# Layer 1 of a two-layer backbone: output weights split and stored in the V/z stage, key stores issued behind the last powers, the eighth weight block's splits issued behind evictions

## The chip, the cores and the metric

The kernel runs on one core of a Trainium2 chip. The core has a matrix engine (PE, with its weight loads shown apart as PEld), a vector engine (DVE), a scalar engine (ACT), a general engine (POOL) and SP, which in this kernel only issues DMA transfers. ACT and POOL issue some transfers too. Each engine works through its own instructions in order; a wait holds everything behind it on that engine. The metric is the device time of one execution in microseconds (us).

## The reference, cut to what matters

The program is a backbone of two layers over 2048 latent tokens of width 1024, with 256 context tokens, in float32. The change is in layer 1, which is a neighbourhood attention layer:

```python
def odd_mixer(h, hc, w_in, q_gain, k_gain, rpb, w_out, update_ctx):
    q, k, v, z = jnp.split(jnp.dot(h, w_in), 4, axis=-1)      # 16 heads of 64; likewise for the context tokens hc
    q, k = rms_norm(q, q_gain), rms_norm(k, k_gain)
    o = neighborhood_attention(q, k, v, k_ctx, v_ctx, rpb)     # 8 x 16 window of a 32 x 64 grid, and all 256 context keys
    y = jnp.dot(o * jax.nn.silu(z), w_out)                     # w_out: 1024 x 1024
# after it: x = x + gate * y
```

(`odd_mixer` is shortened here; the context tokens are not updated in the last layer.)

## The kernel before

**Numbers in two parts.** A float32 matrix is used as a sum of a high part (rounded by an ACT copy to the matmul format) and a low part (DVE: original minus high part). A product takes three matmuls: high x high, high x low, low x high (lines L129, L130 and L131). So each weight block has to be split once: a load into a staging tile `wraw`, an ACT copy (L106, out `w0h` to `w3h`), and a DVE subtraction (L391, out `w0l` to `w3l`).

**Stages of layer 1.** Tiles are 128 tokens: 18 of them, the first two being context. `odd_qk` multiplies the tiles with the weight blocks 0 to 3 of `w_od` (512 columns each: two for q, two for k) and at its end with block 4 (half of V) for the last two tiles. `odd_vz` does the rest of blocks 4 and 5 (V) and 6 and 7 (z). Then `odd_attention` runs eight head pairs, j = 0 to 7, some 47 us each, and ends with the output projection, token tile by token tile.

**`odd_qk`.** A cell is one token tile times one block, 24 matmuls into a PSUM tile `gm`. For q and k: ACT squares (`osq`), DVE sums (`oss`), POOL raises to the power -1/2 (`rpow`, L208 and L210), DVE multiplies (`onat`, L1159), PE transposes (L1167, `tp`), ACT and DVE split the result (`oqh`, `oql`; for keys also `okt`). For V (j = 4) ACT copies `gm` to `onat`, and POOL stores it (`store_v`). The keys are collected for groups of four token tiles in `okt` tiles. When a group is full, POOL stores it to DRAM (`store_k`, L1200): eight transfers of 512 KB for each of the four groups. A transfer that POOL issues stands in POOL's queue with its powers.

**Weight splits on the side.** Lists of steps wait in `self.ahead`. `pump` is called after each step of the matmul stream, and at every fourth call takes one step of the first list: two 128 x 512 pieces of a block. When the last cell of a block is done, `done(j)` appends the next block for the same buffers (blocks 4 to 7 go to the places w0 to w3). The staging tiles `wraw` have three buffers, so a load on SP waits until an earlier split is done. `held(steps)` runs steps so that what they issue comes behind the instruction in `self.evicted`.

**The order of instructions** on each engine is set by a planner. It works with estimated costs; `issue_after(x)` tells it to place what follows behind instruction x.

**`odd_vz`.** `weave` runs the V and z cells and, beside them, `maxes`: for 16 heads, PE multiplies queries with keys (`mx`), DVE adds a table of position biases (`mtab`, to which POOL has added a mask, L1279 and L1280) and takes the largest score of each row. SP loads the keys (`mk`, L1276), tables (L1278) and queries (`mq`, L1288); ACT reorders the queries (`mz`). `gm` has two banks here, `mx` five. The pools of this stage use the SBUF space of the pools of `odd_qk`.

**`odd_attention`.** For each head pair there are 16 latent steps (kind "l") and 4 context steps. Scores go to PSUM (`st`, L1390 and L1391), DVE adds the table (L1548, out `opt`), ACT exponentiates, PE multiplies with the values (`o`, L1402 and L1424), POOL sums the exponentials (`oacc`, L1430). `finish` divides by the sum and stores the result `rc` to the DRAM scratch `RT1`, by POOL. In the last pair, j = 7, the generator `weights` loads the output weights, 512 KB for each k of 0 to 7, into `opt` slots (of which there are 11), and `split` makes the two parts of them: 16 ACT copies and 16 DVE subtractions (L1075), each behind an exponential. The parts go to `wo0` and to buffers that are free by then: old q tiles, `ov`, `tab` and `kc` tiles. For the first token tile, z and all eight rows of `RT1` are loaded at n = 11, multiplied at n = 14 (L1578), split at n = 14 (ACT, `hi0`) and n = 15 (DVE, L1581, `lo0`); the projection begins with `first`.

Of the kernel before, what the change touches and what calls it, by code (L numbers as in the profile page):

```python
# [10 lines left out]
F32 = mybir.dt.float32  # L11
F32R = mybir.dt.float32r
# [5 lines left out]
P = 128  # L18
# [70 lines left out]
class Kern:  # L89
# [115 lines left out]
    def rpow(self, out, in_, mul, add):  # L205

        g = self.nc.gpsimd
        g.tensor_scalar(out=out, in0=in_, scalar1=mul, scalar2=add, op0=ALU.mult, op1=ALU.add)  # L208
        shp = list(out.shape)
        g.tensor_tensor(out=out, in0=out, in1=self.mhalf[:, : shp[1]], op=ALU.pow)  # L210

# [910 lines left out]
    def odd_qk(self, ws, win, hT):  # L1122
# [6 lines left out]
        with ExitStack() as es:  # L1129
# [5 lines left out]
            self.ahead += [self.od_steps(win, 0, ws), self.od_steps(win, 1, ws)]  # L1135
            pend, kt = [], {}

            def cell(t, j):
# [17 lines left out]
                nc.vector.tensor_reduce(out=ss[:], in_=sq[:].rearrange("p (h d) -> p h d", h=8), axis=AX.X, op=ALU.add)  # L1156
                self.rpow(ss[:], ss[:], 1.0 / 64, EPS)
                n = self.tl(sp, [P, 512], "onat", bufs=4)
                nc.vector.tensor_tensor(out=n[:].rearrange("p (h d) -> p h d", h=8), in0=ps[:],  # L1159
                                        in1=ss[:].unsqueeze(2).to_broadcast([P, 8, 64]), op=ALU.mult)  # L1160
                pend.append((t, j, n))

            def fin(t, j, n):
# [29 lines left out]
                if r0 == 6:  # L1193
                    store_k(kt.pop(j), j0, CTX + g * 512, 512)

            def store_k(parts, j0, o, w):

                for u, x in enumerate(parts):
                    for i in range(2):
                        nc.gpsimd.dma_start(self.K1t[j0 : j0 + 4, i, u * 64 : u * 64 + 64, o : o + w].rearrange("j d t -> d j t"),  # L1200
                                            x[i * 64 : i * 64 + 64].bitcast(F32))
# [22 lines left out]
    def odd_vz(self, ws, win, hT):  # L1224
        nc = self.nc
        self.z1 = self.scr("z1", (KD, P, SEQ), F32)
        self.M1 = self.scr("M1", (16, SEQ), F32)
        NR, NC = (len(b) for b in BLOCKS["q"])
        with ExitStack() as es:
# [6 lines left out]
            def cell(t, j):  # L1236
# [6 lines left out]
                if j < 6:  # L1243
                    self.act(n[:], ps[:])
                    self.store_v(t, j - 4, n)
                    return
# [24 lines left out]
            def maxes():  # L1271
# [51 lines left out]
    def odd_attention(self, out, right, left, wout):  # L1323
# [4 lines left out]
        with ExitStack() as es:  # L1328
# [109 lines left out]
            def weights():  # L1438

                for k in range(KD):  # L1440
                    if k == 0:
                        pl = [self.tl(left, [P, D], f"wo0{z}", F32R, bufs=1)[:] for z in "hl"]
                    elif k < 5:
                        q = qtile(8, k % 2, (k + 1) // 2)
                        pl = q[:, :D], q[:, D:]
                    elif k == 5:
                        v = self.tl(vp[0], [P, NT, P], "ov", F32R, bufs=1)[:].rearrange("p t d -> p (t d)")
                        pl = v[:, :D], v[:, D : 2 * D]
                    elif k == 6:
                        pl = [self.tl(tp[0], [P, NR, NC], f"tab{i}", F32R, bufs=1)[:].rearrange("p r c -> p (r c)")[:, :D] for i in range(2)]  # L1450
                    else:
                        pl = None
                    for n in range(2):
                        c = slice(n * 512, n * 512 + 512)
                        if pl:
                            wout[k, n] = [x[:, c] for x in pl]
                        else:
                            k1 = self.tl(kcp, [P, 2, CTX], "kc1", F32R, bufs=2)
                            wout[k, n] = [x[:].rearrange("p i c -> p (i c)") for x in (k1, ones["kc"].pop(0))]
# [15 lines left out]
            Q, kc, kt, V, tabs, raw = {}, {}, [], {}, {}, {}  # L1475
            Q[0, 1] = query(0, 1)
# [9 lines left out]
            mask(tabs[0])  # L1486
            out_w, out_s = weights(), split()
            pend, late, OA, first_sums = [], [], {}, {}
            FIRST_SUMS = {2: 1, 3: 1, 4: 0, 5: 0, 8: 2, 9: 2, 12: 3, 13: 3}
            all_k = slice(0, KD)  # L1490

            def flush(n):

                mm = None
                for f, *a in pend[:n]:
                    mm = f(*a)
                del pend[:n]
                for x in late:
                    x[0] -= 1
                for x in [x for x in late if x[0] <= 0]:  # L1500
                    late.remove(x)
                    finish_block(*x[1:])
                return mm

            for j in range(8):
                OA[j] = {}, {}
                for s, (kind, n) in enumerate(steps):
# [53 lines left out]
                    pend.append((tail_ctx if kind == "c" else tail, n, pts, j, V[j], *OA[j]))  # L1561
                    if j == 7 and 3 < s < 17:
                        with self.tc.issue_after(ex.ins):
                            next(out_s, None)
                    if j == 7 and n == 11:
                        z0, r0 = [exps([P, KD, P]) for _ in range(2)]
                        rows(z0, self.z1, 0, all_k)
                        rows(r0, self.RT1, 0, all_k)
                    elif j == 7 and n == 12:
# [4 lines left out]
                        hi0, lo0 = [exps([P, KD, P], F32R) for _ in range(2)]  # L1574
                    elif j == 7 and n in (14, 15):
                        with self.tc.issue_after(bias.ins):
                            if n == 14:
                                nc.vector.tensor_tensor(out=r0[:], in0=r0[:], in1=z0[:], op=ALU.mult)  # L1578
# [158 lines left out]
```

## Time and profile before

| | |
|---|---|
| median of 3 runs | 3652.93 us (3652.69 to 3655.3) |
| the profiled execution | 3652.31 us; span 3650.5 us; mean granted PE clock 0.988 |
| PE busy | 3552.0 us (97%), 18404 matmuls |
| DVE busy | 2355.2 us (65%) |
| ACT busy | 1433.2 us (39%) |
| POOL busy | 1234.9 us (34%) |
| `odd_qk` ends, `odd_vz` begins | 2621.0 us from the span's start |
| first matmul of the maxima | 2641.0 us |
| first matmul of the output projection | 3459.7 us |

The views show, for each engine, what was busy and what ended an idle time. In a timeline, a line has the start and the duration in us, the engine, the source line, the operation, out<-in, the shapes, and in brackets the idle time of that engine just before, with what released it. A matmul's duration overlaps with its neighbours; the distance from start to start is the pace. In a line of the waits stand the engine, its line, what it waited for, and the total, the number and the longest of these waits. In a line of the windows stand the stretch, its length, the busy time and number of instructions of PE, PEld, DVE, ACT and POOL, the clock that PE was granted (1.00 is full), the busy share of the 16 DMA engines, and GB/s.

### The profile page before, as it was taken

How to read it: one execution, taken by the hardware profiler on the slowest of the kernel's cores; microseconds unless marked ns; L12 is line 12 of the kernel's file. 1: busy time of each engine (PE TensorE's matmuls, PEld its weight loads, DVE VectorE, ACT ScalarE, POOL GpSimd, SP SyncE). 2: the span in 40 equal slices, each digit the busy share in tenths (PEclk: the TensorE clock that was granted, in tenths of full speed). 3: DMA queues.
4: the chain of work that ended last, by engine and by line, in shares of the span. 5: the costliest groups of instructions: out<-in, count | busy, mean ns of one | idle time of the engine just before them, and what ended most of it. 6: DMA issues, size and time to landing. Idle time of an engine off the chain costs nothing. (4 is left out here: it accounts for less than half of the span.)

```text
span 3650.5 us, 51811 instructions
## 1 busy us (share of the span) xinstructions
PE 3552.0 (97%) x18404; PEld 2747.6 (75%) x18404; DVE 2355.2 (65%) x4846; ACT 1433.2 (39%) x2740; POOL 1234.9 (34%) x1376
## 2 busy tenths in 40 slices
PE   8999999999999999999999999999899999999899
PEld 6988987888886666665656887888788887555577
DVE  4677666888876766678765435455488784666732
ACT  5445551111115555555654214444422222555510
POOL 1433330101011211221311224333344442888763
PEclk9999999999999999999999999999999999999999
DMA  7455463222243232342632544545734446898672
GB/s 259 142 156 155 135 177 110 87 75 84 69 116 86 66 107 66 89 125 66 179 110 93 184 139 141 159 146 155 245 126 144 131 133 181 212 223 220 190 235 97
DMA packets 365780, 512.25 MB, mean 140 GB/s; under 512 B 26081, under 2 KB 245297, under 8 KB 359618
## 3 DMA queue, kind: packets, MB, share of 16 engines
q1 hardware_dynamic: 320754, 417.69, 39.3%
q0 software_dynamic: 22112, 63.26, 5.7%
q10 hardware_dynamic: 22656, 27.99, 2.2%
q8 instruction: 146, 2.39, 0.3%
q14 instruction: 112, 0.92, 0.1%
HBM read 329.45 MB, written 179.37 MB: 139 GB/s over the span
## 5 line engine op out<-in xcount | busy, mean ns | idle before, releaser
L963 DVE TENSOR_TENSOR acc<-acc,apt 128x512 f32<-128x512 f32 x512 | 375.6, 756 | 168.5 <-ACT apt L106 165.6
L106 ACT ACTIVATE apt<-st 128x512 f32<-128x512 f32 (+1 forms) x592 | 343.6, 594 | 290.7 <-PE st L974 262.0
L660 DVE TENSOR_REDUCE mm<-mx 128x1 f32<-128x512 f32 (+1 forms) x656 | 388.7, 629 | 87.3 <-PE mx L659 80.0
L914 PE MATMUL av<-apt,av 128*64 128x512 f32 (+1 forms) x1184 | 280.6, 594 | 0.0
L972 PE MATMUL st<-aq,akh 97*128 97x512 f32 (+1 forms) x592 | 256.6, 434 | 8.8 <-DMA aq<-QT 4.4
L659 PE MATMUL mx<-mk,mq 96*128 96x512 f32 (+1 forms) x656 | 235.8, 373 | 5.0 <-DMA mq<-QT 3.4
L1430 POOL TENSOR_TENSOR oacc<-oacc,opt 128x576 f32<-128x576 f32 (+5 forms) x192 | 223.0, 1184 | 39.7 <-ACT rl L106 19.3
L973 PE MATMUL st<-aq,akh 96*128 96x512 f32 (+1 forms) x592 | 235.5, 398 | 0.0
L1548 DVE TENSOR_TENSOR opt<-st,tab 128x64 f32<-128x64 f32 (+10 forms) x576 | 144.6, 317 | 140.3 <-PE st L1391 63.8
L974 PE MATMUL st<-aq,akl 96*128 96x512 f32 (+1 forms) x592 | 234.4, 396 | 0.0
L106 ACT ACTIVATE u<-gm 128x352 f32<-128x352 f32 (+1 forms) x140 | 68.6, 498 | 373.2 <-PE gm L131 210.6
L1307 DVE CUSTOM_DVE_ANT_1 mx<-mx,mtab 128x217 f32<-128x217 f32 (+12 forms) x576 | 184.2, 338 | 40.1 <-PE mx L1301 30.9
L914 PEld LDWEIGHTS av<-apt,av 128*64 128x64 f32 x1184 | 80.5, 137 | 153.6 <-issue 152.3
L972 PEld LDWEIGHTS st<-aq,akh 97*128 97x128 f32 x592 | 113.0, 191 | 99.1 <-issue 50.5
L106 ACT ACTIVATE opt<-opt 128x930 f32<-128x930 f32 (+7 forms) x129 | 104.2, 810 | 110.7 <-DVE opt L1548 102.6
L659 PEld LDWEIGHTS mx<-mk,mq 96*128 96x128 f32 x656 | 121.2, 188 | 16.8 <-DMA mk<-KT 3.8
L974 PEld LDWEIGHTS st<-aq,akl 96*128 96x128 f32 x592 | 113.9, 193 | 25.6
L973 PEld LDWEIGHTS st<-aq,akh 96*128 96x128 f32 x592 | 114.4, 193 | 17.1
L129 PE MATMUL gm<-w1h,hhi 128*128 128x512 f32 x288 | 116.3, 404 | 6.8 <-ACT onat L106 6.8
L106 ACT ACTIVATE x<-px,modB,modA 128x128 f32<-128x128 f32 x272 | 99.3, 468 | 56.9 <-PE px L339 54.4
L129 PE MATMUL gm<-w0h,hhi 128*128 128x512 f32 x288 | 116.3, 404 | 2.0 <-DVE hhi L351 1.9
L807 POOL TENSOR_TENSOR gsf<-gsf,D 64x512 f32<-64x512 f32 x17 | 25.1, 1477 | 271.4 <-DVE D L784 271.4
(492 smaller groups left out, 9962.1 us busy)
## 6 DMA issues: line engine op xcount, KB each, us to landing
q<-Q SPq DMA_DIRECT2D x48, 512.0 KB
H<-x ACTq DMA_DIRECT2D x36, 512.0 KB
adaw<-ada_w SPq DMA_DIRECT2D x64, 256.0 KB
x<-H SPq DMA_DIRECT2D x32, 512.0 KB
wraw<-w_od SPq DMA_DIRECT2D x64, 256.0 KB
K1t<-okt POOLq DMA_DIRECT2D x32, 512.0 KB, 7.6
kt<-K1t SPq DMA_DIRECT2D x32, 512.0 KB
mtab<-rpb_q SPq DMA_DIRECT2D x16, 899.0 KB
```

Of the source, the lines that this page charges most:

```text
L106: return self.nc.scalar.activation(out, in_, func, **kw)
L129: self.nc.tensor.matmul(out, lh(k), rh(k), start=j == 0, stop=False)
L659: mm = nc.tensor.matmul(ps[:, :w], q[:A_QK, (t % 6) * P : (t % 6) * P + P], k[:A_QK, k0 : k0 + w], start=True, stop=True)
L660: nc.vector.tensor_reduce(out=m[:, t, n : n + 1], in_=ps[:, :w], axis=AX.X, op=ALU.max)
L914: nc.tensor.matmul(O[j, nb][i * 64 : i * 64 + 64, :w], V[j, kt // TT][:, kt % TT, i * 64 : i * 64 + 64], pts[i][:, :w], start=n == 0, stop ...
L963: nc.vector.tensor_tensor(out=acc[i][:, :w], in0=a[:, :w], in1=pts[i][:, :w], op=ALU.add)
L972: nc.tensor.matmul(ps[:, :w], kh[: A_QK + 1, i, kq], qh[: A_QK + 1, :w], start=True, stop=False)
L973: nc.tensor.matmul(ps[:, :w], kh[:A_QK, i, kq], ql[:A_QK, :w], start=False, stop=False)
L974: mm = nc.tensor.matmul(ps[:, :w], kl[:A_QK, i, kq], qh[:A_QK, :w], start=False, stop=True)
L1307: nc.vector.tensor_tensor_reduce(out=s, in0=s, in1=tb[:, ri : ri + rn, ci : ci + cn], scale=1.0, scalar=-3e38, op0=ALU.add, op1=ALU.max, a ...
L1430: self.psum = nc.gpsimd.tensor_tensor(out=a, in0=a, in1=pts[:, :, a0 - r0 : a1 - r0, :], op=ALU.add)
L1548: bias = nc.vector.tensor_tensor(out=pt[:, d[0], d[1]], in0=ps[:, d[0], d[1]], in1=tabs[j][i][:, ri : ri + rn, ci : ci + cn], op=ALU.add)
```

## The change

There are three parts.

1. In `odd_qk`, the eight key stores of the last group (g = 3) are kept in a list `last` and issued behind the power of the last cell, (17, 1); `rpow` returns that instruction. The splits of the eighth block (j = 7, place w3) come from `late()`: four empty steps, then `held`, so that they stand behind the V copies (`self.evicted`, set in `odd_qk` and `odd_vz`).
2. In `odd_vz`, a new generator `output_weights` is appended to `self.ahead`. After 16 empty steps it loads 16 pieces of 128 x 512 of the output weights (256 KB each, into `wraw` tiles), splits each by an ACT copy and a DVE subtraction, and has POOL store both parts to a DRAM scratch `WO`; five empty steps follow each piece.
3. In `odd_attention`, j = 7, `split` is gone. `weights` loads both parts from `WO` straight to their places (8 MB in all instead of 4 MB). For the first token tile only the rows k < 7 are loaded from `RT1` and multiplied, at n = 13; the last eighth is taken from the tile that `finish` returns (`done_rows[0, 7]`), at n = 14, ahead of `hi0`.

```diff
-        g.tensor_tensor(out=out, in0=out, in1=self.mhalf[:, : shp[1]], op=ALU.pow)
+        return g.tensor_tensor(out=out, in0=out, in1=self.mhalf[:, : shp[1]], op=ALU.pow)
...
-                    self.act(n[:], ps[:].rearrange("p h d -> p (h d)"))
+                    self.evicted = self.act(n[:], ps[:].rearrange("p h d -> p (h d)"))
...
+                if (t, j) == (NT - 1, 1):
+                    with self.tc.issue_after(power.ins):
+                        for x in last:
+                            store_k(*x)
...
                 if r0 == 6:
-                    store_k(kt.pop(j), j0, CTX + g * 512, 512)
+                    last.append((kt.pop(j), j0, CTX + g * 512, 512))
+                    if g < 3:
+                        store_k(*last.pop())
...
+            def late():
+                yield from range(4)
+                yield from self.held(self.od_steps(win, 7, ws))
+
             nxt = {2: 4, 3: 5, 0: 6, 1: 7}
-            done = lambda j: j in nxt and self.ahead.append(self.od_steps(win, nxt[j], ws))
+            done = lambda j: j in nxt and self.ahead.append(late() if j == 1 else self.od_steps(win, nxt[j], ws))
...
+        self.WO = self.scr("WO", (KD, P, 2, D), F32)
...
+            def output_weights():
+
+                yield from range(16)
+                for k in range(KD):
+                    for n in range(2):
+                        lo, hi = [self.tl(self.prp, [P, 1, 512], "wraw", dt, bufs=self.wbufs) for dt in (F32, F32R)]
+                        c = slice(n * 512, n * 512 + 512)
+                        nc.sync.dma_start(lo[:], self.i["w_out1"][:, k : k + 1, c])
+                        self.act(hi[:], lo[:])
+                        nc.vector.tensor_tensor(out=lo[:].bitcast(F32R), in0=lo[:], in1=hi[:], op=ALU.subtract)
+                        for z, x in enumerate((hi[:].bitcast(F32), lo[:])):
+                            nc.gpsimd.dma_start(self.WO[k, :, z, c], x[:, 0])
+                        yield from range(5)
+
+            self.ahead.append(output_weights())
...
                     if k == 0:
-                        pl = [self.tl(left, [P, D], f"wo0{z}", F32R, bufs=1)[:] for z in "hl"]
+                        x = self.tl(left, [P, 2, D], "wo0", F32R, bufs=1)[:]
...
+                    if k < 6:
+                        self.load(x.bitcast(F32), self.WO[k])
+                        x = [x[:, 0], x[:, 1]]
...
-                    raw[k] = exps([P, D])
-                    self.load(raw[k][:], self.i["w_out1"][:, k, :])
...
-            def split():
-                for k in range(KD):
-                    for n in range(2):
-                        hi, lo = wout[k, n]
-                        self.project_split(raw[k][:, n * 512 : n * 512 + 512], hi, lo)
-                        wout[k, n] = [x.unsqueeze(1) for x in (hi, lo)]
-                        yield
...
-                    finish_block(*x[1:])
+                    done_rows[tuple(x[1:3])] = finish_block(*x[1:])
...
-                    if j == 7 and 3 < s < 17:
-                        with self.tc.issue_after(ex.ins):
-                            next(out_s, None)
...
-                        rows(r0, self.RT1, 0, all_k)
+                        rows(r0, self.RT1, 0, most_k)
...
-                    elif j == 7 and n in (14, 15):
+                    elif j == 7 and n in (13, 14, 15):
                         with self.tc.issue_after(bias.ins):
-                            if n == 14:
-                                nc.vector.tensor_tensor(out=r0[:], in0=r0[:], in1=z0[:], op=ALU.mult)
+                            if n == 13:
+                                nc.vector.tensor_tensor(out=r0[:, most_k, :], in0=r0[:, most_k, :], in1=z0[:, most_k, :], op=ALU.mult)
+                            elif n == 14:
+                                nc.vector.tensor_tensor(out=r0[:, KD - 1, :], in0=done_rows[0, 7][:, :P], in1=z0[:, KD - 1, :], op=ALU.mult)
                                 self.act(hi0[:], r0[:])
...
-            for _ in out_s:
-                pass
```

On the engines' queues, the change leaves the number of matmuls and the order of most instructions as they were. At the end of `odd_qk` POOL has all powers first, then the eight key stores, then the V stores; ACT has the eight splits of block 6 (`w2h`) ahead of the last two `onat` copies and those of block 7 (`w3h`) behind them. In `odd_vz` the first matmuls of the maxima stand behind 39 instead of 29 matmuls with w2, and the 32 stores to `WO` fall into the first five of the sixteen heads. In j = 7 SP issues 12 loads from `WO` instead of 8 of `w_out`.

More of the change, by code (lines that the diff above doesn't have):

```diff
@@ L1135, in odd_qk @@
             self.ahead += [self.od_steps(win, 0, ws), self.od_steps(win, 1, ws)]
[L1136 removed]
+            pend, kt, last = [], {}, []
             def cell(t, j):
@@ L1449, in weights @@
+                    if k < 6:
+                        self.load(x.bitcast(F32), self.WO[k])
+                        x = [x[:, 0], x[:, 1]]
                     elif k == 6:
-                        pl = [self.tl(tp[0], [P, NR, NC], f"tab{i}", F32R, bufs=1)[:].rearrange("p r c -> p (r c)")[:, :D] for i in range(2)]
-                    else:
-                        pl = None
+                        x = [self.tl(tp[0], [P, NR, NC], f"tab{i}", F32R, bufs=1)[:].rearrange("p r c -> p (r c)")[:, :D] for i in range(2)]
+                        for z in range(2):
+                            self.load(x[z].bitcast(F32), self.WO[k, :, z])
@@ L1472, in rows @@
+                        k1 = self.tl(kcp, [P, 2, CTX], "kc1", F32R, bufs=2)
+                        x = [y[:].rearrange("p i c -> p (i c)") for y in (k1, ones["kc"].pop(0))]
+                        for z in range(2):
+                            self.load(x[z].bitcast(F32), self.WO[k, :, z, c])
+                        wout[k, n] = [y.unsqueeze(1) for y in x]
+                    yield
             def rows(tile, RT, o, ks):
                 self.load(tile[:, ks, :], RT[ks, :, o * P : o * P + P].rearrange("j p t -> p j t"))
-            Q, kc, kt, V, tabs, raw = {}, {}, [], {}, {}, {}
+            Q, kc, kt, V, tabs = {}, {}, [], {}, {}
@@ L1486, in odd_attention @@
             mask(tabs[0])
-            out_w, out_s = weights(), split()
-            pend, late, OA, first_sums = [], [], {}, {}
+            out_w = weights()
+            pend, late, OA, first_sums, done_rows = [], [], {}, {}, {}
             FIRST_SUMS = {2: 1, 3: 1, 4: 0, 5: 0, 8: 2, 9: 2, 12: 3, 13: 3}
-            all_k = slice(0, KD)
+            all_k, most_k = slice(0, KD), slice(0, KD - 1)
             def flush(n):
```

17 lines of the change are left out of this document (7 added, 10 removed).

## The prediction

> **What bounds the kernel now.** I read the page's first part (busy time by engine), then the chain of waits of TensorE over the span, then the timelines around the two places that the change touches, and the windows of the stage between them.
>
> ```profile
> span 3650.5 us, 51811 instructions
> PE 3552.0 (97%) x18404; PEld 2747.6 (75%) x18404; DVE 2355.2 (65%) x4846; ACT 1433.2 (39%) x2740; POOL 1234.9 (34%) x1376
> ...
> PE gm L129 <- ACT onat L106: 6.8, 1, 6.8
> PE st L129 <- ACT opt L106: 6.3, 1, 6.3
> ```
>
> TensorE is the bound: 3650.5 - 3552.0 leaves 98.5 us without a matmul, and the number of matmuls does not change. So a gain can only be idle time of PE, or time in which its clock is low. In the waits (total, times, longest) two single stalls stand out, 6.8 and 6.3 us. The first is where the query/key stage ends and the V/z stage begins, the second where the last head ends and the output projection begins. The change works on these two places, and pays in the stage between.
>
> **Part A, the boundary (key stores deferred, eighth weight block held).** Timelines of PE, POOL and ACT (start, duration, engine, operation, idle before):
>
> ```profile
> 2600.10 0.78 PE L1167 MATMUL tp<-ident,onat 128*128 128x128 f32 x4 [1.94 <-DVE onat L1159]
> 2601.96 0.63 PE L129 MATMUL gm<-w0h,hhi 128*128 128x512 f32 x1
> 2604.44 0.40 PE L130 MATMUL gm<-w0l,hhi 128*128 128x512 f32 x1
> 2620.98 0.79 PE L129 MATMUL gm<-w1h,hhi 128*128 128x512 f32 x1 [6.77 <-ACT onat L106]
> 2624.13 0.48 PE L130 MATMUL gm<-w1l,hhi 128*128 128x512 f32 x1
> ...
> 2594.59 1.31 POOL L1200 DMA_DIRECT2D K1t<-okt  x2 [9.11 <-ACT okt L106]
> 2596.28 1.26 POOL L1200 DMA_DIRECT2D K1t<-okt  x2
> 2597.56 1.67 POOL L210 TENSOR_TENSOR oss<-oss,mhalf 128x8 f32<-128x8 f32 x1
> 2605.40 1.64 POOL L210 TENSOR_TENSOR oss<-oss,mhalf 128x8 f32<-128x8 f32 x1
> ...
> 2609.65 0.63 ACT L106 ACTIVATE w2h<-wraw 128x512 fp32r<-128x512 f32 x1 [5.47 <-DMA wraw<-w_od]
> 2620.35 0.58 ACT L106 ACTIVATE onat<-gm 128x512 f32<-128x512 f32 x1
> ...
> 2600.00:2605.00 5.00, 4.90 (x17) 4.04 (x18) 1.86 (x4) 1.70 (x3) 1.23 (x1) 0.66 1.06 318
> 2640.00:2650.00 10.00, 8.48 (x41) 6.45 (x40) 5.78 (x5) 5.26 (x8) 9.30 (x3) 1.00 0.56 224
> ```
>
> POOL stood 9.11 us on a key store, waiting for okt, and a power (L210) was queued behind it and behind the two issues at 2596.28; the normalised tile then came 1.94 us late for the transposes. With the eight stores behind the last power, that wait goes: 1.94 us. The copy onat, which frees the PSUM bank for the first w1 matmul, stands in ScalarE's queue behind the w2 splits, which wait for weight loads while the DMA engines are full (share 1.06, the column before GB/s). Of the 8 stores of 512 KB, 4 MB, none moves in this time now. At some 300 GB/s (318 in that window) that is 13 us of transfer time for the w2 loads to use. In the new order all w2 splits stand ahead of the last two onat copies, no w3 split does. I take it that the copy comes when PE is done; left is the copy, 0.58, and handing over, together 0.9. Gain 6.77 - 0.9 = 5.9.
>
> After both gaps the matmuls took 0.63 us each instead of 0.40 (the rows at 2601.96 and 2604.44), for about 3.5 and 3.1 us (to the row at 2624.13). With the clock at about half in that time, 1.6 + 1.5 = 3.1 us are lost to it. A gap of 0.9 costs no clock: the window 2640:2650 holds one of 0.96 us at clock 1.00. Sum so far 1.94 + 5.9 + 3.1 = 10.9.
>
> What is late next: the first key block of the row maxima is loaded through SP into memory that the key tiles occupy, so SP must wait until the deferred stores have landed; behind it the score table and the first queries.
>
> ```profile
> 2628.50 0.33 SPq L1276 DMA_DIRECT2D mk<-K  x1
> 2640.96 0.38 PE L1294 MATMUL mx<-mk,mz 128*128 128x256 f32 x1 [0.55 <-ACT mz L106]
> ...
> K1t<-okt POOLq DMA_DIRECT2D x8, 512.0 KB, 7.7
> ```
>
> The last power ends near 2607; eight issues of 0.66 take until 2612.3, and 7.7 us to landing (the last row) gives 2620. The mk load, which SP reaches behind seven w3 loads, would be at 2628.5 less the 8 us gained, 2620.5: hardly later. From its issue to the maxima's first matmul are 12.5 us now, so about 2633. PE would be there at 2640.4 - 10.9 + 2.3 (ten more weight matmuls ahead of it in the new order, 0.23 each) = 2631.8. I charge 3 us for the stall and for the 4 MB now running beside these loads. A: 10.9 - 3 = 8. Ends: 0 (the loads stay as late as they are) and 10.9.
>
> **Part B, the output weights split in the V/z stage.** Sixteen pieces of 256 KB: a load, one ACT copy, one DVE subtraction, two POOL stores of 256 KB. Windows of the first part of that stage (PE, PEld, DVE, ACT, POOL busy, clock, DMA share, GB/s) and rows for the prices:
>
> ```profile
> 2660.00:2700.00 40.00, 40.00 (x203) 33.67 (x202) 32.46 (x144) 11.03 (x18) 11.33 (x10) 1.00 0.43 144
> 2700.00:2740.00 40.00, 40.00 (x197) 33.49 (x197) 29.91 (x126) 10.82 (x20) 22.79 (x20) 1.00 0.43 134
> 2740.00:2780.00 40.00, 40.00 (x202) 33.55 (x201) 32.02 (x146) 11.32 (x19) 14.84 (x12) 1.00 0.45 137
> ...
> L391 DVE TENSOR_TENSOR w3l<-wraw,w3h x8: 619/693/2609, 2621.5 to 2648.5; 128x512 fp32r<-128x512 f32 x8
> L1222 POOL DMA_DIRECT2D V<-ovz x20: 523/546/580, 2672.5 to 2794.1; - x20
> DMA to landing us min/median/max: 2.2/2.5/5.3
> ...
> ACT ovz L106 <- PE gm L131: 28.6, 12, 6.3
> ```
>
> In these 120 us PE is never idle. Sixteen copies of 0.63 add 10 us to ACT's 33; 32 issues of 0.55 add 17.6 to POOL's 49; 12 MB over some 130 us add 92 GB/s to 140. All this fits. DVE is the narrow place: 94.4 of 120 us busy, and 16 subtractions cost 11 us at the median of 0.69, or 42 us if each took the longest time, 2.6. That would be 16 us more than the 120 hold (94.4 + 42). POOL is busy only 49 of the 120 us, so I take the low price. The Trainium skill (SBUF — State Buffer, "SBUF: two separate sides") says that a VectorE instruction with two SBUF inputs and a GpSimd one that reads SBUF lock each other out for a whole instruction. The spread from 0.62 to 2.61 fits that; if every piece met POOL's table work, it would be the 16 us.
>
> The other cost is order. A piece's copy waits in ACT's queue for its load and for an earlier piece's stores to land (2.2 to 5.3 us), in front of the evictions that PE's two banks need; its load waits in SP's queue in front of the next queries. ACT came 2.4 us early to an eviction on average (28.6 / 12). So a hold of 2 to 3 us is hidden and one of 5 is not. With bounds of 0 and 16 x (5.3 - 2.4) = 46 us, I take 2 us, near the low end, as PE showed no wait at all in this stage.
>
> **Part C, last head and output projection.** Groups and timelines:
>
> ```profile
> 3410.00:3455.00 45.00, 38.35 (x240) 22.91 (x238) 43.65 (x84) 27.17 (x44) 35.51 (x30) 0.91 0.48 150
> 3340.00:3390.00 50.00, 48.83 (x351) 29.73 (x349) 30.75 (x90) 27.15 (x42) 43.41 (x40) 1.00 0.88 223
> 3430.00:3440.00 10.00, 9.45 (x56) 6.71 (x58) 9.63 (x17) 7.12 (x13) 10.00 (x9) 0.67 0.42 119
> 3455.00:3460.00 5.00, 0.34 (x1) 0.34 (x2) 3.77 (x10) 1.42 (x2) 2.29 (x2) 0.50 1.05 351
> ...
> 3430.55 0.80 PE L1390 MATMUL st<-q,kc 128*128 128x512 f32 x1 [1.35 <-ACT opt L106]
> 3451.42 0.40 PE L1390 MATMUL st<-q,kt 128*128 128x352 f32 x1 [2.48 <-DVE opt L1548]
> 3459.66 0.80 PE L129 MATMUL st<-wo0h,opt 128*128 128x512 f32 x1 [6.25 <-ACT opt L106]
> ...
> 3464.05 0.39 PE L129 MATMUL st<-q,opt 128*128 128x512 f32 x1
> ...
> 3449.53 2.40 DMA RT<-rc
> 3452.02 4.01 DMA opt<-RT
> 3456.12 2.35 DVE opt L1578
> 3458.55 1.07 ACT opt L106
> ```
>
> In the last head DVE is full, 43.65 of 45 us, against 30.75 of 50 in the head before; the sixteen subtractions of L1075 make the difference, and they go, with sixteen ACT copies of 0.62. So the waits 1.35 and 2.48 go. The last rows are the chain into the projection: the last eighth's result is stored, read back with the other seven, multiplied, split. Now only the other seven are read, earlier; the last goes from SBUF into a product of 128 columns. Of 6.25 us stays what follows the last scores: the bias, ACT's copy of 1.07, together 1.5. Idle gained: 1.35 + 2.48 + 4.75 = 8.6. Behind the 1.35 gap the clock fell: in 3430:3440 PE was busy for 9.45 us at a mean clock of 0.67, so 9.45 x 0.33 = 3.1 us are lost; this goes too. After the 6.25 gap nine matmuls took 4.4 us (3459.66 to 3464.05) instead of the 2.1 of nine at 0.23; a gap of 1.5 is like the 1.35 that did slow the clock, so these 2.3 stay. C: 11.7, less 0.7 for more transfers, 11. The Trainium skill (TensorE: Matmul & The Clock Gate, "What's actually happening") has the half clock only after an idle window of about 3.4 us. By that, the gaps of 1.94 and 1.35 us would have cost no clock, so 1.6 of A and 3.1 of C would not be there to gain, 2.3 more would, and the time would be 3638.4. The rows at 2601.96 and 3430 show slow matmuls behind just these gaps, so the trace disagrees and the rule gets no chance of its own.
>
> Against it: loads of 1 MB replace those of 512 KB, 4 MB more over the last head, in front of the last key chunks in SP's queue. At 150 GB/s in use and 351 in the fullest window there is room. If they come late, the 6.25 stays and C is 4: the lower end; the upper is 8.6 + 3.1 + 2.3, 14.
>
> **Sum.** 8 - 2 + 11 = 17 us off the profiled execution's 3652.31, that is 3635.3. This execution lies 0.6 us under the median of 3652.93, so 3636 for the median.
>
> **Rivals.** (1) ACT still waits for the w2 loads, now with the last square (osq) behind all eight splits: A gives 2, the time is 3642. For it: ACT waited 5.47 us on one load; against it: the key stores' 4 MB are out of the way. (2) The output weights or the seven eighths land late: C gives 4, time 3643. For it: DMA share above 1 at 3455. (3) Slower: the pieces' copies hold ACT's queue in the V/z stage. It decides from 19/16 = 1.2 us of PE time for each piece; at 1.7 us it costs 27 us and the time is 3661. For it: store landings up to 5.3 us, and only two gm banks; against: ACT is idle 87 of 120 us, and its waits for mq cost PE nothing now. (4) DVE runs short of time in that stage, 16 us by the longest subtraction: 19 gained, 16 lost, 3650. For it: DVE is busy 79% there; against it: the median of 0.69.
>
> **How the numbers follow.** The forecast has 0.56, (1) 0.14, (2) 0.12, (3) 0.10, (4) 0.08. About 0.2%, 7.3 us, can be told from no change: forecast, (1) and (2) are faster by more, 0.82; (4) is the same, 0.08; (3) slower, 0.10. The forecast's own range is 3629 to 3643: A between 4 and 10.9, B between 0 and 5, C between 8 and 14. For 8 in 10 the range reaches over (1) and (2) and to the edge of (4): 3627 to 3650.
>
> **What would show it.** Right: no PE wait over 1.5 us at the first w1 matmul and at the transposes before it, clock 1.00 there; PE 40.00 of 40 in the windows of the V/z stage; DVE under 35 of 45 us in the last head, and the projection's first matmul waiting under 2 us. Wrong: waits of gm on ovz or of mx on mz in the V/z stage; w2 splits still waiting for loads when PE is done; the projection waiting for WO.

## The result and the profile after

The changed kernel takes 3659.38 us (median of 20 executions, 3653.40 to 3664.64), the one before 3654.10 us (20 executions, 3650.21 to 3663.81). The ratio is 1.0013, with an interval of 1.0007 to 1.0019: about 5 us slower. The forecast was 3636. The profiled execution of the changed kernel took 3653.4 us, so it lies 6 us under its median; the profiled one of before lies 1.8 us under the median of these 20. The two traces therefore differ by only 1.1 us of span; the other 4 us or so between the medians lie in no stretch that the traces show. I use the traces, one execution of each kernel, for places, and the ratios for verdicts.

Three stretches divide the trace: from the first w0 matmul of the query/key stage to the first w1 matmul of the V/z stage; from there to the first scores of the attention; from there to the first matmul of the output projection.

| us | to the first w1 matmul | V/z stage | eight head pairs | span |
|---|---|---|---|---|
| before | 369.1 | 461.3 | 377.3 | 3650.5 |
| after | 359.7 | 484.3 | 365.6 | 3651.6 |
| difference | -9.4 | +23.0 | -11.7 | +1.1 |

(What lies ahead of the first stretch is 0.7 us shorter.)

Both stalls named in the prediction went, and a stretch in which PE had hardly waited lost more than both. First TensorE's waits after the change, from 2040 us on (engine, line, what it waited for: total, number, longest):

```profile
PE gm L129 <- ACT ovz L106: 10.3, 1, 10.3
...
PE mx L1305 <- ACT mz L106: 2.5, 2, 1.8
...
PE mx L1312 <- DVE mm L1318: 2.3, 2, 1.5
PE st L129 <- ACT opt L106: 2.2, 1, 2.2
PE tp L1262 <- DVE ovz L1259: 2.1, 1, 2.1
...
PE mx L1312 <- DVE mm L1307: 2.0, 1, 2.0
PE mx L1305 <- DVE mm L1318: 1.8, 1, 1.8
...
PE gm L129 <- ACT onat L106: 0.7, 1, 0.7
```

The wait on `onat` fell from 6.8 to 0.7 us and the one in front of the projection from 6.3 to 2.2. New are 10.3 us on `ovz`, a V eviction. The waits on `mz`, on `mm` and of `tp` add up to 10.7 us, where the kernel before had 2.4 of them.

The large one in the changed kernel's timelines of PE, ACT, POOL and SP (start, duration; in brackets the idle time before and its releaser):

```profile
2610.84 0.50 PE L129 MATMUL gm<-w1h,hhi 128*128 128x512 f32 x1 [0.69 <-ACT onat L106]
2632.38 0.80 PE L129 MATMUL gm<-w2h,hhi 128*128 128x512 f32 x1 [10.28 <-ACT ovz L106]
2646.53 0.39 PE L1305 MATMUL mx<-mk,mz 128*128 128x256 f32 x1 [1.80 <-ACT mz L106]
...
2610.69 1.66 ACT L106 ACTIVATE w3h<-wraw 128x512 fp32r<-128x512 f32 x3
2631.22 0.63 ACT L106 ACTIVATE w3h<-wraw 128x512 fp32r<-128x512 f32 x1 [18.87 <-DMA wraw<-w_od]
2631.75 0.58 ACT L106 ACTIVATE ovz<-gm 128x512 f32<-128x512 f32 x1
...
2606.52 5.09 POOL L1206 DMA_DIRECT2D K1t<-okt  x8
...
2612.07 20.86 SPq L388 DMA_DIRECT2D wraw<-w_od  x4
...
2633.70 1.79 SPq L1287 DMA_DIRECT2D mk<-K  x1
```

And in its windows (length, busy time of PE, PEld, DVE, ACT, POOL, clock, DMA share, GB/s):

```profile
2600.00:2605.00 5.00, 4.84 (x24) 3.72 (x23) 3.75 (x6) 4.02 (x7) 0.26 (x2) 1.00 0.59 155
...
2615.00:2620.00 5.00, 5.00 (x24) 4.10 (x23) 0.00 (x0) 0.00 (x0) 1.06 (x3) 1.00 1.03 369
...
2625.00:2630.00 5.00, 0.00 (x0) 0.00 (x0) 0.00 (x0) 0.00 (x0) 0.00 (x0) 0.50 0.78 240
2630.00:2635.00 5.00, 2.62 (x6) 2.13 (x7) 2.69 (x6) 2.64 (x5) 1.89 (x4) 0.50 0.29 84
2635.00:2640.00 5.00, 5.00 (x16) 3.91 (x16) 1.96 (x5) 1.91 (x2) 0.18 (x1) 0.68 0.94 308
```

The first w1 matmul comes 10 us earlier than before. POOL issues the eight deferred stores, 4 MB, from 2606.5 to 2611.6. Three w3 loads were issued ahead of them; the fourth comes behind them, at 2612.07 (the first of the four issues in the SP row). The DMA engines are full (share 1.03 in 2615 to 2620), and that load of 256 KB lands just before 2631.2, 19 us after its issue. Its split stands in ScalarE's queue ahead of the first `ovz` eviction, a copy of 0.58 us; both `gm` banks stay occupied, and PE stands still for 10.3 us. After it the clock is 0.50 and 0.68: 2.62 x 0.50 + 5.00 x 0.32 = 2.9 us more. The key block `mk` is loaded at 2633.7 instead of 2628.5, and the maxima begin at 2646.5 instead of 2641.0, although PE had been 10 us ahead.

Of the smaller ones, the 2.5 us on `mz` and the 1.8 on `mm` come before 2657, where queries and tables land late; they are still there (2.0 and 1.9) in the run below that takes the subtractions from DVE and keeps the deferred stores. The other 6.4 us come from DVE. The changed kernel's subtractions of the pieces as a group (number: least, median, longest ns, first and last start):

```profile
L1338 DVE TENSOR_TENSOR wraw<-wraw,wraw x16: 679/694/3933, 2656.3 to 2789.4; 128x512 fp32r<-128x512 f32 x16
```

Two of the long ones in its timelines of DVE, POOL and PE:

```profile
2656.34 3.93 DVE L1338 TENSOR_TENSOR wraw<-wraw,wraw 128x512 fp32r<-128x512 f32 x1
2736.20 3.16 DVE L1338 TENSOR_TENSOR wraw<-wraw,wraw 128x512 fp32r<-128x512 f32 x1
2739.28 0.68 DVE L1307 TENSOR_REDUCE mm<-mx 128x2 f32<-128x512 f32 x1
...
2656.00 3.71 POOL L1291 TENSOR_TENSOR mtab<-mtab,maskq 128x1798 f32<-128x1798 f32 x1
2735.61 3.20 POOL L1290 TENSOR_TENSOR mtab<-mtab,maskq 128x1798 f32<-128x1798 f32 x1 [5.79 <-DVE mm L1318]
...
2740.01 0.49 PE L1312 MATMUL mx<-mk,mz 128*128 128x480 f32 x1 [2.01 <-DVE mm L1307]
```

The median is what I had taken, 0.69 us. But a subtraction that begins beside one of POOL's table additions (3.2 or 3.7 us) ends 0.55 us after that addition: at 2660.27 and 2739.36, after 3.93 and 3.16 us. In the whole trace six of the sixteen took over 2 us. A reduction that frees a bank of the maxima stands behind it, and PE waits 2.0 us for that. The Trainium skill (SBUF — State Buffer, "SBUF: two separate sides") has it that a VectorE instruction with two SBUF inputs and a GpSimd one that reads SBUF lock each other out for a whole instruction; these rows agree.

The last head after the change, in the stretch that is shown of before:

```profile
3410.00:3455.00 45.00, 43.77 (x284) 25.82 (x282) 29.60 (x86) 25.18 (x40) 36.73 (x35) 1.00 0.85 295
```

And the projection's start in the timeline of PE:

```profile
3460.74 0.71 PE L129 MATMUL st<-wo,opt 128*128 128x512 f32 x1 [2.21 <-ACT opt L106]
```

DVE has 29.6 us of work in 45 instead of 43.65, PE 43.8 instead of 38.4, the clock is 1.00 instead of 0.91, and the projection's first matmul waits 2.2 us instead of 6.3.

### The profile page after: what moved, and what is told of

Its sections match the earlier page's. It is cut to its first block, busy times and chain, and to the rows that moved or that the text cites. A ratio compares the mean times of both kernels' runs of the same rounds, so it can differ in the third digit from the quotient of the medians.

```text
span 3651.6 us, 51894 instructions
## 1 busy us (share of the span) xinstructions
PE 3550.4 (97%) x18404; PEld 2746.0 (75%) x18404; DVE 2354.1 (64%) x4847; ACT 1431.2 (39%) x2740; POOL 1241.7 (34%) x1408
## 4 chain that ended last, share of the span: by engine, by line
PE 83%; DMA 6%; DVE 5%; POOL 2%; issue 2%; ACT 2%; SPq 0%; DVEq 0%; ACTq 0%; POOLq 0%
PE gm L129 9%; PE gm L130 9%; PE gm L131 9%; PE av L914 7%; PE st L972 4%; PE mx L659 4%; PE st L973 3%; PE st L974 3%; PE st L1416 2%; PE o L1450 2%; PE pj L129 2%; PE pj L130 2%; PE pj L131 2%; PE st L131 2%; PE st L129 2%
## 5 line engine op out<-in xcount | busy, mean ns | idle before, releaser
L972 PE MATMUL st<-aq,akh 97*128 97x512 f32 (+1 forms) x592 | 256.5, 433 | 10.9 <-DMA aq<-QT 5.9
L1318 DVE CUSTOM_DVE_ANT_1 mx<-mx,mtab 128x217 f32<-128x217 f32 (+13 forms) x576 | 183.3, 339 | 29.8 <-PE mx L1312 20.4
```

The costliest lines, as they stand in the source:

```text
L972: nc.tensor.matmul(ps[:, :w], kh[: A_QK + 1, i, kq], qh[: A_QK + 1, :w], start=True, stop=False)
```

## Experiments

Two reasons had to be told apart for the loss in the V/z stage. Theory 1 is that the deferred 4 MB make the w3 loads late, and the eviction behind their splits late with them. The other is that the subtractions on DVE meet POOL's table additions. A third, general answer was that a stall taken away there only moves. Each ratio is against the kernel before on the same chip, with its 95% interval; where the interval holds 1.0000, the run does not tell the kernel from the one before. The stretches come from one trace of each kernel. Executions of one kernel spread over 7 to 18 us, so a difference of a few us between two stretches is a hint, and a named wait in the trace weighs more.

**One part at a time.** The second and third part without the first:

```diff
-                if (t, j) == (NT - 1, 1):
-                    with self.tc.issue_after(power.ins):
-                        for x in last:
-                            store_k(*x)
...
-                    if g < 3:
-                        store_k(*last.pop())
+                    store_k(*last.pop())
...
-            done = lambda j: j in nxt and self.ahead.append(late() if j == 1 else self.od_steps(win, nxt[j], ws))
+            done = lambda j: j in nxt and self.ahead.append(self.od_steps(win, nxt[j], ws))
```

> Leaves out the first part of the change (key stores and the eighth block stay as before); the output weights are split and stored in the V/z stage and read back in the last head. Theory 1, the key stores: the changed kernel's 10.3 us wait (weight matmuls on the copy ovz) comes from the deferred stores filling the DMA engines. Then that wait is gone here, the 6.8 us wait on onat at the boundary is back, the pieces cost about 9.6 us of the V/z stage (22.9 us between the first w1 matmul and the last head minus 13.3 until the first maxima), the last head and the projection gain 11.7: about 2 us faster than before. Theory 2, the pieces: their loads and ACT copies make the whole loss of 22.9 us in the V/z stage; then this kernel is about 11 us slower than before and shows the wait of 10 us on ovz.

Measured: 0.9996 (0.9988 to 1.0005), 3653.03 us against 3654.69. The three stretches take 369.9, 469.5 and 363.9 us. The wait on `onat` is back (7.2), none is on `ovz`. The eight head pairs keep their whole gain, 13.4 us, and the V/z stage gives 8.2 of it back. TensorE's waits in this kernel, from 2590 to 2900 us:

```profile
PE tp L1253 <- DVE ovz L1250: 3.6, 1, 3.6
PE mx L1303 <- DVE mm L1298: 2.7, 1, 2.7
```

Timelines of DVE and POOL:

```profile
2649.36 4.15 DVE L1329 TENSOR_TENSOR wraw<-wraw,wraw 128x512 fp32r<-128x512 f32 x1
2735.88 3.17 DVE L1329 TENSOR_TENSOR wraw<-wraw,wraw 128x512 fp32r<-128x512 f32 x1
...
2735.30 3.20 POOL L1281 TENSOR_TENSOR mtab<-mtab,maskq 128x1798 f32<-128x1798 f32 x1 [5.81 <-DMA mtab<-rpb_q]
```

The last two rows overlap as in the changed kernel. So by the traces the pieces alone cost some 8 us, without any deferred store.

The first part alone, with the output weights as before:

```diff
-        self.WO = self.scr("WO", (KD, P, 2, D), F32)
...
-            self.ahead.append(output_weights())
...
-            out_w = weights()
+            out_w, out_s = weights(), split()
```

> Only the first part of the change (key stores behind the last powers, eighth block held); output weights as before. Theory 1, the key stores: the first w1 matmul comes about 10 us earlier than before, then a wait of about 10 us on ovz while a w3 split waits for its load some 18 us, first maxima some 3 us later than before; 3 us slower in all. Theory 2, the pieces: no wait on ovz, the 10 us of the boundary stay gained, about 3642 us.

Measured: 1.0004 (0.9995 to 1.0014), 3655.11 us. Stretches 361.8, 472.9 and 377.5 us. The timeline of PE:

```profile
2633.45 0.79 PE L129 MATMUL gm<-w2h,hhi 128*128 128x512 f32 x1 [10.40 <-ACT ovz L106]
2647.17 0.39 PE L1304 MATMUL mx<-mk,mz 128*128 128x256 f32 x1 [2.17 <-ACT mz L106]
```

In this timeline of PE the `ovz` wait is the same (10.40 against 10.28) without any output weights in the stage. The boundary gains 7.3 us and the V/z stage gives back 11.6. The eight pairs are as before, 377.5: their gain belongs to parts two and three alone.

**Inside the first part.** The stores in their old place, the held block kept:

```diff
-                    if g < 3:
-                        store_k(*last.pop())
+                    store_k(*last.pop())
```

> The changed kernel without the deferral: key stores where they were, eighth block still held, output weights as changed. Theory 1, the key stores: no wait over 4 us on ovz; the waits at the boundary are those of before (1.9 and 6.8); pieces cost 9.6, the end gains 11.7: 0 to 4 us faster than before. Theory 3, the held order: a w3 split at the head of ACT's queue in front of the eviction makes the wait, with or without the stores; then 8 to 10 us on ovz stay, and the time is some 6 us above before.

Measured: 0.9990 (0.9981 to 0.9998), 3651.69 us. The wait on `ovz` is gone, `onat` is back at 7.8. Against the changed kernel's 1.0013 this one edit is worth 0.23%, 8 us, and the intervals do not meet: deferring the stores is what makes the change a loss.

The other way round, stores deferred, the eighth block's splits not held:

```diff
-            done = lambda j: j in nxt and self.ahead.append(late() if j == 1 else self.od_steps(win, nxt[j], ws))
+            done = lambda j: j in nxt and self.ahead.append(self.od_steps(win, nxt[j], ws))
```

> The changed kernel with the key stores deferred but the eighth block's splits not held: w3 splits then stand ahead of the two onat copies. Theory 1, the key stores: the w3 load that lands late now holds the copy onat, so the wait moves to the first w1 matmul, 8 to 15 us, and there is none on ovz; 0 to 6 us slower than before. Theory 3, the held order: with w3 splits no longer in front of the eviction ovz no wait over 3 us at either place, and 6 to 10 us faster than before.

Measured: 1.0007 (0.9997 to 1.0016), 3658.7 us. The timeline of PE:

```profile
2633.34 0.80 PE L129 MATMUL gm<-w1h,hhi 128*128 128x512 f32 x1 [19.06 <-ACT onat L106]
```

The wait goes to the eviction before, `onat`, and grows to 19 us. So `held` does move the splits past one eviction; with the loads as late as they are, PE only gets on to the next eviction with it. The V/z stage takes 463.0 us here, only 1.7 more than before, although DVE subtracts the pieces and five of the sixteen subtractions take 1.6 to 3.5 us; PE's waits on the maxima add up to 3.5 us. So in these traces a long subtraction has no fixed price.

Half of the stores deferred, those of one of the two key blocks, 2 MB:

```diff
-                    if g < 3:
+                    if g < 3 or j == 2:
                         store_k(*last.pop())
```

> The changed kernel, but of the eight key stores only the four of block 3 (2 MB) are deferred; the four of block 2 are issued where they were. Theory 1, the deferred bytes fill the DMA engines when the w3 loads need them: half the bytes, so the late w3 load lands before the first V eviction needs ACT; the wait on ovz falls from 10.3 to 0 to 3 us, the boundary keeps 7 to 10 us of its gain, some 8 to 12 us faster than the changed kernel, 4 to 9 faster than before. Theory 4, not the bytes but that any store is queued there: the wait stays at 8 to 10 us.

Measured: 1.0005 (0.9995 to 1.0015), 3661.12 us. The `ovz` wait is 4.5 us, where 0 to 3 was expected, and the gain did not come. Another wait came in, as timelines of PE and DVE show:

```profile
2658.32 1.12 PE L1262 MATMUL tp<-ident,ovz 128*128 128x128 f32 x4 [6.08 <-DVE ovz L1259]
...
2650.04 7.63 DVE L391 TENSOR_TENSOR w3l<-wraw,w3h 128x512 fp32r<-128x512 f32 x2 [1.36 <-ACT w3h L106]
```

Two w3 subtractions take 7.63 us of DVE, while POOL adds tables from 2649.36 to 2657.13; behind them stands the product that makes `ovz`, and PE waits 6.1 us for its transposes. These are not the pieces: the held block's own subtractions have come among POOL's table additions.

**The subtractions on POOL.** From the weights-only kernel, one word:

```diff
-                        nc.vector.tensor_tensor(out=lo[:].bitcast(F32R), in0=lo[:], in1=hi[:], op=ALU.subtract)
+                        nc.gpsimd.tensor_tensor(out=lo[:].bitcast(F32R), in0=lo[:], in1=hi[:], op=ALU.subtract)
```

> The kernel with the output weights alone (first part of the change left out), with the sixteen subtractions of the pieces on POOL instead of DVE. Theory 5, subtractions on DVE that run beside POOL's table additions take 3 to 4 us and hold the maxima: the 8 us that the pieces cost between the first w1 matmul and the first scores of the attention fall to 0 to 3, no PE wait over 1 us there after 2660. Theory 6, the pieces' copies and loads hold ACT's and SP's queues: the 8 us stay, or grow by POOL's longer queue.

Measured: 0.9974 (0.9964 to 0.9985), 3647.06 us against 3656.75. Stretches 367.4, 459.5 and 366.7. The subtractions as a group, with 15 of the 16 pieces in the stretch from 2640 to 2800 us:

```profile
L1329 POOL TENSOR_TENSOR wraw<-wraw,wraw x15: 1277/1293/1683, 2651.2 to 2790.5; 128x512 fp32r<-128x512 f32 x15
```

Windows of the V/z stage in this kernel:

```profile
2660.00:2700.00 40.00, 40.00 (x203) 33.74 (x202) 31.28 (x146) 13.52 (x23) 21.86 (x24) 1.00 0.65 214
2700.00:2740.00 40.00, 40.00 (x198) 33.52 (x198) 30.61 (x127) 13.40 (x23) 32.00 (x31) 1.00 0.63 209
2740.00:2780.00 40.00, 40.00 (x201) 33.49 (x200) 32.57 (x141) 11.78 (x20) 21.85 (x21) 1.00 0.71 210
```

On POOL a subtraction takes 1.3 us, twice DVE's 0.69, but it cannot meet POOL's own table work. PE is never idle in these 120 us; in the changed kernel it was busy for 39.31, 37.25 and 39.99. The V/z stage is 10.0 us shorter than with DVE subtracting, and 1.8 us shorter than before, where a remainder of 0 to 3 us was expected. The loads, 16 copies, stores and DMA traffic of the pieces all remain, so the 8 us came from having the subtractions on DVE and not from these. One reservation: the planner also puts some copies and stores at other places when the engine of the subtractions changes, and no run separates that from the engine alone. This trace is the fastest of its kernel's 12 executions, 7.8 us under their median; by the ratios the edit is worth 0.22%, 8 us, and the two intervals do not meet. This version is faster than both kernels.

**Evictions first.** If the w3 splits stand ahead of the first eviction, six empty steps instead of four might put them behind it:

```diff
             def late():
-                yield from range(4)
+                yield from range(6)
                 yield from self.held(self.od_steps(win, 7, ws))
```

> The changed kernel with six instead of four empty steps ahead of the eighth block's splits, so that the first V eviction stands ahead of all w3 splits on ACT, and the next ones ahead of the splits whose loads come late. Theory 1 in its order form (the late load does harm only because its split stands in front of an eviction): the wait on ovz is gone, but keys, tables and w3 still land late, so a wait of 2 to 8 us shows at the first maxima or w3 matmuls; 2 to 8 us faster than the changed kernel. Theory 4: PE waits as long in all, 12 us, at the maxima or at w3; same as the changed kernel.

Measured: 1.0007 (0.9997 to 1.0017), 3658.82 us: no gain. TensorE's waits in this kernel from 2590 to 2900 us:

```profile
PE mx L1305 <- ACT mz L106: 6.4, 1, 6.4
PE mx L1312 <- DVE mm L1318: 4.8, 3, 2.9
...
PE gm L129 <- ACT ovz L106: 2.0, 1, 2.0
PE gm L130 <- DVE w3l L391: 1.6, 1, 1.6
```

And the second eviction in its timeline of ACT:

```profile
2636.18 0.60 ACT L106 ACTIVATE ovz<-gm 128x512 f32<-128x512 f32 x1 [10.10 <-DMA V<-onat]
```

The first eviction now comes when PE is done, and the `ovz` wait falls to 2.0. But ScalarE stands 10.1 us in front of the second one for a V store, which POOL issues behind the key stores; the maxima start at 2649.1 and wait 6.4 for their queries, and PE now waits for the splits themselves. So a late split is not the only way by which the deferred stores reach the evictions. The stage takes 484.2 us, as in the changed kernel. In these traces the order in ScalarE's queue decides where PE stops, the transfers decide for how long.

**POOL subtracting in the other orders.** The same one-word edit in the kernel with half the stores deferred, in the changed kernel, and in the one with the held block and no deferral.

> Half the key stores deferred and the sixteen subtractions on POOL, the rest as in the changed kernel. If the two causes are separate, their effects add: 4 to 9 us from the first and 5 to 8 from the second, 10 to 16 us faster than before. If the pieces' cost is queueing, no more than the run with half the stores deferred.

Measured: 0.9989 (0.9979 to 1.0000), 3653.26 us; `ovz` wait 6.1, and again a 6.1 us wait behind two w3 subtractions (7.49 us). Less gain than expected, for the reason seen with half the stores.

> The changed kernel with the pieces' subtractions on POOL. With the two causes separate: the wait of about 10 us on ovz stays (key stores), the waits of the maxima on DVE after 2652 go, and the time is 5 to 9 us below the changed kernel's, 2 to 6 below before. If the subtractions on DVE did harm only together with late tables, nothing changes against the changed kernel.

Measured: 0.9987 (0.9978 to 0.9996), 3649.05 us against 3654.2. The `ovz` wait stays at 9.7 us; the V/z stage takes 473.6 us instead of 484.3. So in the changed kernel itself DVE's subtractions are worth some 10 us (10.7 by the stage, 0.26% by the ratios, whose intervals do not meet). The other 12 us of the stage's loss come with the first part, which alone made the stage 11.6 us longer.

> Key stores where they were, eighth block held, subtractions on POOL: the kernel with the output weights and subtractions on POOL, plus the held block. If holding the block is worth something by itself: up to 4 us faster than without it, 12 to 16 us faster than before. If it is worth nothing: 8 to 12 us faster than before, with the waits 1 to 2 and 5 to 8 us at the boundary as there.

Measured: 0.9984 (0.9974 to 0.9995), 3649.83 us. Less than the 8 to 12 us expected, and its interval overlaps that of the best kernel (0.9964 to 0.9985), so the runs don't separate them. The two traces do show a cost: the V/z stage takes 467.0 us against 459.5, with 6.2 us of waits of `mx` and `tp` against 0.3. Timelines of DVE and PE:

```profile
2650.21 7.31 DVE L391 TENSOR_TENSOR w3l<-wraw,w3h 128x512 fp32r<-128x512 f32 x2 [2.42 <-ACT w3h L106]
...
2658.27 1.09 PE L1257 MATMUL tp<-ident,ovz 128*128 128x128 f32 x4 [2.60 <-DVE ovz L1254]
```

In the kernel before, two w3 subtractions meet POOL's table work as well, at 2.6 and 2.4 us; held, two come one behind the other and take 7.3.

This run also limits what the place of the subtractions is worth. Against the same order with DVE subtracting (0.9990) it gains 0.06%, 2 us, and the intervals overlap; the stage is 5.6 us shorter. With half the stores deferred the step from DVE to POOL gains 0.16%, with intervals that still overlap a little, and the stage only 1.9 us. So it is clear in two of four orders.

The `ovz` wait by what is deferred, over the kernels that hold the block by four empty steps: 10.3, 10.4 and 9.7 us with 4 MB, 4.5 and 6.1 with 2 MB, none with nothing deferred. It follows the bytes, whatever the output weights do. (With six steps and 4 MB it is 2.0, and the time goes into the other waits shown above.)

## Why the prediction was wrong

The total was 23 us too low and outside its range; two terms of the sum, A and B, were mis-sized. By the traces A is a loss of some 2 us (10.1 gained up to the first w1 matmul, 12.3 lost in the V/z stage with POOL subtracting), B a loss of 10.7 and C a gain of 11.7, together the 1.1 us by which the traces differ.

- **Part A, the two waits and the clock (10.9 us): right.** The transposes' wait went from 1.94 to 0.16 us, `onat` from 6.8 to 0.7, the clock in 2600 to 2605 is 1.00. The first w1 matmul came 10.1 us earlier, 9.4 of it within the stretch; the 1.5 us of clock behind it are the rest of the 10.9.
- **Part A, "I charge 3 us for the stall and for the 4 MB now running beside these loads": the step that failed.** I asked what is late next, and followed SP's loads to the maxima, not ACT's queue to the next eviction. I had noted that no w3 split stands ahead of the `onat` copies, and did not ask which eviction they stand ahead of: the first `ovz`. The transfer time that I gave the w2 loads as free was taken from the w3 loads. Measured: 10.3 us of wait, 2.9 us of clock, and maxima that begin 5.6 us later instead of 8 earlier. The stores took 10.7 us to land instead of the 7.7 that I carried over, and `mk`, which SP issues behind the w3 loads, was issued at 2633.7 instead of 2620.5; its 12.5 us to the first maxima stayed, 12.8. The first part alone gave +0.04%, not told from no change, instead of -0.2%. The lower end, 0, was also too high: I took "the loads stay as late as they are" as the worst, and they became later.
- **Part B, 2 us: mis-sized, about 10 in this kernel.** I took the 11 us of DVE's subtractions at their median to fit in, because POOL was busy for only 49 of 120 us, and charged 2 us for the order alone. Three things were missed. POOL's work comes in blocks of 3.2 and 3.7 us, one after another, and a share of busy time says nothing of how long one meeting lasts. And a late subtraction is no matter of DVE's total time: the reductions that free the maxima's banks stand behind it. And the trace of before had a nearer price, in the last head, where POOL was busy for 35.51 of 45 us: the same sixteen subtractions of the output weights took 0.68 to 2.28 us there, and the eight that write q tiles had a median of 1.27 (row below this list). Rival (4) had the mechanism and sized it at the sum over all sixteen; six were long, and moving all of them to POOL brought some 10 us.
- **Rival (3), the pieces' copies holding ACT's queue:** not seen. With the copies and transfers still there and the subtractions on POOL, PE was never idle in 2660 to 2780.
- **Rival (1):** the last w2 split began at 2601.9, so it fell as stated; the same mechanism came one block and one eviction later.
- **Part C, 11 us: right.** 11.7 us in the changed kernel, 7.7 to 13.4 in the nine others with these parts, none in the one without. The remaining wait was 2.2 us, not 1.5. Rival (2) fell: the weights were there in time. The lower end of C, 4, was lower than its own terms: with the 6.25 staying, these (1.35, 2.48 and 3.1, less 0.7) give 6.2.
- **The chances.** 0.82 on faster came from three cases that all kept B at 2 us and a positive A. The case that came true, a slower B and a negative A together, was in none; the traces of before had 6.8 us of PE waiting on a copy behind a late load, and that this would come again behind the next late load was a mechanism to list.

The kernel before, subtractions of the last head that write q tiles (number: least, median, longest ns, first and last start):

```profile
L1075 DVE TENSOR_TENSOR q<-opt,q x8: 677/1265/2280, 3423.3 to 3440.2; 128x512 fp32r<-128x512 f32 x8
```

## What to carry to other kernels

A burst of stores that is moved out of the way of one group of loads is in the way of the next group: follow the moved bytes until they have landed, and in each queue look for the next short eviction that stands behind an instruction waiting for a load. Before putting a two-input SBUF operation on DVE, look how long GpSimd's single instructions are in that stretch, not how busy it is; where GpSimd has time to spare, an operation of its own at twice the duration can be cheaper; it clearly was in two of the four orders here. Parts two and three without the first, with the subtractions moved to POOL, are faster than before by 0.26%.

## What the runs showed of the hardware

A load of 256 KB took 19 us from its issue, while 369 and 240 GB/s were moving in the two windows shown of that time. A subtraction of 0.69 us lasted up to 4.15 us beside POOL's additions, and two of the w3 block together up to 7.63.

Not expected was how unevenly the clock answers to short gaps. After the changed kernel's gap of 2.01 us, which ends at 2740.01, the pace was full at first and then halved; after the one of 2.10 us, which ends at 2797.08, it did not fall:

```profile
2740.34 0.39 PE L129 MATMUL gm<-w1h,hhi 128*128 128x512 f32 x1
2740.57 0.55 PE L130 MATMUL gm<-w1l,hhi 128*128 128x512 f32 x1
2740.92 0.63 PE L131 MATMUL gm<-w1h,hlo 128*128 128x512 f32 x1
...
2797.08 0.66 PE L1262 MATMUL tp<-ident,ovz 128*128 128x128 f32 x4 [2.10 <-DVE ovz L1259]
2797.74 0.40 PE L129 MATMUL gm<-w0h,hhi 128*128 128x512 f32 x1
2797.97 0.40 PE L130 MATMUL gm<-w0l,hhi 128*128 128x512 f32 x1
```

(Timeline of PE, changed kernel.) From start to start it is 0.23 us, then 0.35, and 0.42 from 2740.92 on in the one, and 0.23 in the other. So the length of the gap alone does not decide whether the clock falls; what else does, no run here shows. Here the slow stretch costs an estimated 1.6 us: the clock is 0.96 over the 40 us from 2740.
